# One layer on one core: projections on 512 columns, four and three counts in the top-k, first expert weights split on ScalarE and VectorE

## The chip, the core and the metric

The kernel runs on one core of a Trainium2 chip. The time is device microseconds of one execution. Of the kernel before, three runs gave 3871.36, 3886.71 and 3886.52 us, a median of 3886.52 us.

## The reference

One layer of a diffusion backbone: 2048 latent tokens and 256 context tokens of 1024 channels, all in float32. The line of computation that matters here:

```python
h_lat, h_ctx = modulate(layer_norm(x), sh1, sc1), modulate(layer_norm(ctx), mc[0], mc[1])
mix = token_mixer(h_lat, h_ctx, ...)     # p = h @ w_in; attention on part of p's columns,
                                         # RWKV-7 scans on the others; concat(...) @ w_out
x = layer_norm_affine(ALPHA * x + gt1 * mix, ln1_g, ln1_b)
h2 = modulate(layer_norm(x), sh2, sc2)
aff = softmax(h2 @ router_w)             # 2048 tokens x 16 experts
gate, idx = top_k(aff.T, 256)            # each expert takes its 256 best tokens
xin = h2[idx]                            # 16 x 256 x 1024
y = (silu(xin @ w_gate) * (xin @ w_up)) @ w_down
x = layer_norm_affine(ALPHA * x + gt2 * scatter_add(gate * y), ln2_g, ln2_b)
```

The six modulation vectors (sh1, sc1, ...) come from `silu(c) @ w_ada + b_ada`.

## The kernel before

**A product in float32** is made of three matmuls. `split` (its cast is at line 43 when it goes to ScalarE, at line 45 on GpSimd; its subtraction at line 48, on VectorE) makes of an operand a high part of fewer bits and a low part, the rest: `wh` and `wl` of weights `wf`, `hTh` and `hTl` of tokens, `xh` and `xl` of an expert's tokens. The product sums high x high, high x low and low x high over 8 blocks of 128 channels: 24 matmuls into one accumulator.

**Stages**, by the profiled execution. Up to some 660 us the input projection, then the mixers until 2383, the output projection until 2613, the router with its top-k until 2683, the gather of the first expert's tokens, sixteen experts to some 3696, 70 us each, and the last normalisation.

**Input projection.** Tokens come in 9 tiles of 256 (t = 0 is the context). `to_hT` transposes a tile (16 transposes, line 307), modulates it (line 315) and splits it into `hT` of 8 x 256 columns. Weights come in column pieces of 256. Seven pieces (p = 3 to 9) go through `piece_ch` channel by channel: for each of three groups of three tiles, each tile and each half of 128 weight columns, 24 matmuls on 256 token columns (line 460, the weights as stationary operand), then a copy into `raw` on ScalarE (line 472), and token shifts and stores from there. The other pieces go through `piece_tok` (line 422), with the tokens as stationary operand. `fill` puts small work between matmuls: the rest of the transposes, and the small products of the modulation weights (line 191), 16 blocks of which are loaded during this stage into the same buffers `wf` by the queue of SyncE, which also issues the pieces' weight loads and the stores (`rkl`, `wll`) of the pieces. A scheduler sets the order on each engine by priorities; each engine takes its work in that order.

**Output projection.** 16 tiles of 128 tokens; `proj` makes for each four accumulations of 24 matmuls on 256 columns of the weights (line 1508, `woh` and `wol`, the tokens `mh`, `ml` as stationary operand), two into each 512-column bank. VectorE and ScalarE normalise behind that, and 8 transposes per tile (line 1551) lead to the router's logits.

**Top-k.** Two searches (`largest`) of five rounds each find the 256th largest value for each expert, three bits a round. In a round, seven candidates are tried at once: VectorE counts for five (line 1689), ScalarE sums signs for two (line 1686); TensorE adds over partitions, the signs first (line 1695), then the counts (line 1696); VectorE makes of that the number of candidates that hold (line 1697), the next candidates (`tkcand`, line 1700, from `tkbase`, line 1692) and the threshold (line 1702). After the first search come lines 1716 and following.

**Experts.** Weights come in pieces of 1 MB into four buffers `wf` and are split into three buffers `wh`, `wl`; the pieces run gate, up, gate, up, ..., then four of down. `fetch` issues a load, `split` the split, `take` both, four and two pieces ahead. The first two pieces are fetched and split ahead of the first expert, the first four are loaded from 2626 us on. Pieces 0 and 1 are cast and subtracted on GpSimd, pieces 2 and 3 cast on ScalarE and subtracted on GpSimd (lines 1843 and 1844), the others go through `split` of line 43. `compact` and `gathered` make the first expert's list of tokens and fetch them.

## Time and profile before

| | us |
|---|---|
| median of three runs | 3886.52 |
| the profiled execution's own time | 3881.74 |
| its span | 3880.0 |
| TensorE busy | 3521.1 (91%) |
| VectorE busy | 2584.3 (67%) |
| ScalarE busy | 1714.7 (44%) |
| GpSimd busy | 1446.5 (37%) |

The profile is of one execution. Busy time is summed over the instructions of an engine; matmuls overlap, so the distance between their starts, not the duration in a row, is what one of them takes from the stream. The granted clock is a share of TensorE's higher level of 2.4 GHz. A chain of waits is followed back from the last instruction; where several instructions follow each other on one engine it gives them as one piece with their count. A row of the timeline gives start, duration, engine, line, operation, the tiles written and read with their shapes, and, in brackets, how long the engine had been idle and what released it.

### The profile page before, as it was taken

How to read it: one execution, taken by the hardware profiler on the slowest of the kernel's cores; microseconds unless marked ns; L12 is line 12 of the kernel's file. 1: busy time of each engine (PE TensorE's matmuls, PEld its weight loads, DVE VectorE, ACT ScalarE, POOL GpSimd, SP SyncE). 2: the span in 40 equal slices, each digit the busy share in tenths (PEclk: the TensorE clock that was granted, in tenths of full speed). 3: DMA queues.
4: the chain of work that ended last, by engine and by line, in shares of the span. 5: the costliest groups of instructions: out<-in, count | busy, mean ns of one | idle time of the engine just before them, and what ended most of it. 6: DMA issues, size and time to landing. Idle time of an engine off the chain costs nothing. (4 is left out here: it accounts for less than half of the span.)

```text
span 3880.0 us, 83041 instructions
## 1 busy us (share of the span) xinstructions
PE 3521.1 (91%) x34103; PEld 2969.3 (77%) x34103; DVE 2584.3 (67%) x4413; ACT 1714.7 (44%) x3255; POOL 1446.5 (37%) x1326
## 2 busy tenths in 40 slices
PE   7999898689998998899999999984999999999987
PEld 6888797466666666666777666983999999999976
DVE  5665646666766777676667766786565555556588
ACT  4544344344444444344454434543444444444443
POOL 3332322465655555565665541333101011011025
PEclk8999998799999999899999998996999999999988
DMA  7756544222232333333224324433667666666674
GB/s 230 240 177 189 161 154 144 65 65 69 71 84 71 91 94 90 90 83 77 68 70 101 83 54 155 149 124 128 216 206 211 213 205 209 213 211 212 211 270 165
DMA packets 635534, 554.78 MB, mean 143 GB/s; under 512 B 264113, under 2 KB 584145, under 8 KB 635153
## 3 DMA queue, kind: packets, MB, share of 16 engines
q1 hardware_dynamic: 622672, 505.94, 42.7%
q0 software_dynamic: 12480, 43.52, 4.8%
q8 instruction: 268, 4.39, 0.5%
q14 instruction: 114, 0.93, 0.1%
HBM read 428.28 MB, written 121.03 MB: 142 GB/s over the span
## 5 line engine op out<-in xcount | busy, mean ns | idle before, releaser
L904 POOL TENSOR_TENSOR acc<-acc,pt 128x512 f32<-128x512 f32 x496 | 660.2, 1331 | 352.4 <-ACT pt L876 327.4
L48 DVE TENSOR_TENSOR wl<-wf,wh 128x1024 fp32r<-128x1024 f32 x434 | 532.5, 1252 | 292.7 <-ACT wh L43 292.5
L1975 PE MATMUL gu<-xh,wl 128*128 128x256 f32 x2048 | 585.7, 286 | 20.9 <-DVE wl L48 20.9
L43 ACT CAST wh<-wf 128x1024 fp32r<-128x1024 f32 x434 | 440.6, 1046 | 333.2 <-issue 105.9
L1975 PE MATMUL gu<-xh,wh 128*128 128x256 f32 x2048 | 582.8, 285 | 0.9 <-DVE sg L1981 0.9
L1975 PE MATMUL gu<-xl,wh 128*128 128x256 f32 x2048 | 583.6, 285 | 0.0
L876 ACT ACTIVATE pt<-st 128x512 f32<-128x512 f32 x576 | 316.7, 595 | 389.9 <-PE st L872 359.5
L843 DVE TENSOR_REDUCE mx<-bk 128x1 f32<-128x512 f32 (+1 forms) x640 | 377.9, 627 | 154.8 <-PE bk L841 153.9
L1975 PEld LDWEIGHTS gu<-xh,wl 128*128 128x128 f32 x2048 | 391.0, 191 | 22.3 <-DVE wl L48 22.3
L1975 PEld LDWEIGHTS gu<-xh,wh 128*128 128x128 f32 x2048 | 392.2, 191 | 1.9 <-DVE sg L1981 1.1
L1975 PEld LDWEIGHTS gu<-xl,wh 128*128 128x128 f32 x2048 | 390.0, 190 | 0.6
L897 PE MATMUL po<-pt,vt 128*64 128x256 f32 x2304 | 320.2, 403 | 1.6 <-ACT pt L876 1.3
L2019 POOL DMA_INDIRECT acc<-ysb,idx x30 | 47.9, 1597 | 680.8 <-DVE ysb L2016 589.6
L460 PE MATMUL mm<-hTh,wh 128*128 128x256 f32 x968 | 281.8, 291 | 4.0 <-POOL raw L479 2.2
L460 PE MATMUL mm<-hTl,wh 128*128 128x256 f32 x968 | 278.8, 288 | 1.2 <-DVE hTl L48 1.2
L460 PE MATMUL mm<-hTh,wl 128*128 128x256 f32 x968 | 276.0, 285 | 0.0
L871 PE MATMUL st<-qs,k 128*128 128x512 f32 x576 | 250.2, 434 | 10.2 <-ACT pt L876 10.1
L872 PE MATMUL st<-q,kl 65*128 65x512 f32 x576 | 236.2, 410 | 11.7 <-DMA q<-mr 11.7
L841 PE MATMUL bk<-k,qs 128*128 128x512 f32 (+1 forms) x640 | 230.7, 440 | 16.5 <-DVE mx L843 7.3
L897 PEld LDWEIGHTS po<-pt,vt 128*64 128x64 f32 x2304 | 145.6, 140 | 104.1 <-issue 45.6
L460 PEld LDWEIGHTS mm<-hTh,wh 128*128 128x128 f32 x968 | 186.6, 193 | 12.4 <-issue 8.1
L460 PEld LDWEIGHTS mm<-hTl,wh 128*128 128x128 f32 x968 | 186.7, 193 | 6.2 <-issue 4.1
(431 smaller groups left out, 8298.7 us busy)
## 6 DMA issues: line engine op xcount, KB each, us to landing
wf<-in_exp_w_gate_dram SPq DMA_DIRECT2D x64, 1024.0 KB
wf<-in_exp_w_up_dram SPq DMA_DIRECT2D x64, 1024.0 KB
wf<-in_exp_w_down_dram SPq DMA_DIRECT2D x64, 1024.0 KB
win<-rkl SPq DMA_DIRECT2D x64, 512.0 KB
wf<-in_w_in_dram SPq DMA_DIRECT2D x30, 1024.0 KB
wf<-in_w_ada_dram SPq DMA_DIRECT2D x20, 1024.0 KB
wl<-wll SPq DMA_DIRECT2D x64, 256.0 KB
pwin<-rkl SPq DMA_DIRECT2D x32, 384.0 KB
```

The lines of the kernel that those rows point to most:

```text
L43: nc.scalar.copy(hi, src)
L48: nc.vector.tensor_sub(lo, src, hi)
L460: mm = nc.tensor.matmul(ps[:, c], a[:, k, cs], b[:, k], start=m == 0, stop=m == 3 * KD - 1)
L841: nc.tensor.matmul(ps[:, :n], qs[:, hh, i * 128:(i + 1) * 128], K2[j][:, c * 512:c * 512 + n], start=True, stop=True)
L843: nc.vector.reduce_max(mx[:, hh * 2 + i, c:c + 1], ps[:, :n], axis=AX.X)
L871: nc.tensor.matmul(st, K2[j][:, ksl], qs, start=True, stop=False)
L872: nc.tensor.matmul(st, KL[j][:, ksl], q2, start=False, stop=True)
L876: nc.scalar.activation(pt, st, AF.Exp, scale=0.125)
L897: nc.tensor.matmul(po[hh * 64:(hh + 1) * 64], VT[j][:, kt], pt[:, hh], start=kt == 0, stop=kt == KT - 1)
L904: add(acc, acc, pt)
L1975: mm = nc.tensor.matmul(ps[:, i], a[:, k, 128 * c:128 * c + 128], b[:, k], start=n == 0, stop=n == 3 * KD - 1)
L2019: nc.gpsimd.indirect_dma_start(out=self.acc, in_=y[h], in_offset=None, compute_op=ALU.add, out_offset=bass.IndirectOffsetOnAxis(ap=idx[h], ...
```

## The change

The input projection's tiles are grouped anew: `GROUPS` names in each of the three groups one tile alone and one pair. The two tiles of a pair lie side by side in one `hT` of 512 columns, and `piece_ch` runs their 24 matmuls on 512 columns (line 464 now) into one bank and copies the whole bank. The small work is put in after the fourth and the eighth block of channels, so that its number of places stays. The spare buffers for the first modulation weights are halves of the new `hT`. In the output projection, weights lie in two tiles of 512 columns and each accumulation runs on 512 (line 1528 now). In the top-k, VectorE counts for four candidates (line 1710 now) and ScalarE sums signs for three (line 1707 now). All expert weights go through `split`, and the first two pieces' splits are written behind the first expert's compaction.

```diff
+            GROUPS = [[(0,), (1, 2)], [(3, 4), (5,)], [(6, 7), (8,)]]
             def hslot(i):
-                return [(htop if i < 3 else hbot).tile([128, KD, 256], F32R, name=f"hT{n}{i}") for n in "hl"]
+
+                if i == 2:
+                    return [htop.tile([128, KD, 256], F32R, name=f"hT{n}2") for n in "hl"]
+                if i in (0, 3):
+                    pair[i] = [(hbot if i else htop).tile([128, KD, 512], F32R, name=f"hT{n}{i}") for n in "hl"]
+                j = i in (1, 4)
+                return [x[:, :, 256 * j:256 * j + 256] for x in pair[i - j]]
...
-                hi, lo = hslot((0, 1, 2, 3, 4, 2, 0, 1, 2)[t])
+                slot = (2, 0, 1, 3, 4, 2, 0, 1, 2)[t]
+                hi, lo = hslot(slot)
...
+                def chain(ps, c, hi, lo):
+                    cs = slice(c * 128, (c + 1) * 128)
+                    m = 0
+                    for k in range(KD):
+                        for a, b in ((wh, hi), (wh, lo), (wl, hi)):
+                            mm = nc.tensor.matmul(ps, a[:, k, cs], b[:, k], start=m == 0, stop=m == 3 * KD - 1)
+                            m += 1
+                        if k == KD - 1 or k == 3 and hi.shape[2] == 512:
+                            fill(mm)
+
+                for n, ts in enumerate(GROUPS[g]):
+                    o = 2 + (512 if n and g else 0)
+                    if len(ts) == 2:
+                        for c in range(2):
+                            ps = pmm.tile([128, 512], F32, name="mm")
+                            chain(ps, c, *H[ts])
+                            nc.scalar.copy(raw[c][:, o:o + 512], ps)
+                        continue
...
-                    for j in (2 * c, 2 * c + 1):
-                        n = 0
-                        o = ps[:, (j % 2) * 256:(j % 2) * 256 + 256]
-                        for k in range(KD):
-                            for a, b in ((hi, woh), (hi, wol), (lo, woh)):
-                                nc.tensor.matmul(o, a[:, k], b[j][:, k], start=n == 0, stop=n == 3 * KD - 1)
-                                n += 1
-                        yield
+                    n = 0
+                    for k in range(KD):
+                        for a, b in ((hi, woh), (hi, wol), (lo, woh)):
+                            nc.tensor.matmul(ps, a[:, k], b[c][:, k], start=n == 0, stop=n == 3 * KD - 1)
+                            n += 1
+                        if k % 4 == 3:
+                            yield
...
-                for j in range(5, 7):
+                for j in range(4, 7):
                     nc.scalar.activation(junks, dh, AF.Sign, bias=cand[:, j:j + 1], scale=-1.0,
...
-                for j in range(5):
+                for j in range(4):
                     nc.vector.tensor_scalar(junk, d, cand[:, j:j + 1], None, op0=ALU.is_ge, op1=ALU.add,
...
-                    if i < 4:
-                        (nc.gpsimd.tensor_copy if i < 2 else nc.scalar.copy)(hi[:, s], w[:, s])
-                        nc.gpsimd.tensor_sub(lo[:, s], w[:, s], hi[:, s])
-                    else:
-                        self.split(hi[:, s], lo[:, s], w[:, s])
+                    self.split(hi[:, s], lo[:, s], w[:, s])
...
-            for i in range(2):
-                split(i)
             c0 = compact(0)
             self.slots(slice(1, NE))
+
+            with tc.issue_after(self.last_compact.ins):
+                for i in range(2):
+                    split(i)
```

The compiled order shows three places where instructions moved. First TensorE at the start of the input projection; `hTh_412` and `hTl_413` are tile 1's `hT`, and `tp<-ident` are the transposes of tile 2, which the kernel before has among tile 1's matmuls:

```order
L307 MATMUL tp<-ident,hTl_150 128x128
L460 MATMUL mm<-hTl_413,wh 128x256
L460 MATMUL mm<-hTh_412,wl 128x256
L460 MATMUL mm<-hTh_412,wh 128x256
L307 MATMUL tp<-ident,hTl_150 128x128 x10
L460 MATMUL mm<-hTl_413,wh 128x256
L460 MATMUL mm<-hTh_412,wl 128x256
```

The same place now, where `hTh_180` and `hTl_181` are the context tile's and `hTh_410` and `hTl_411` the first pair's:

```order
L316 MATMUL tp<-ident,hTh_149 128x128
L464 MATMUL mm<-hTh_180,wh 128x256
L464 MATMUL mm<-hTl_181,wh 128x256
L464 MATMUL mm<-hTh_180,wl 128x256
L316 MATMUL tp<-ident,hTh_149 128x128 x15
L464 MATMUL mm<-hTh_410,wh 128x512 x2
L464 MATMUL mm<-hTh_180,wh 128x256
```

All sixteen transposes of the pair's second tile stand ahead of the pair's first matmul.

Then ScalarE from the softmax of the logits (`lg`) to the split of the first expert's tokens (`xh<-tpe`), before:

```order
L1629 ACTIVATE lg<-lg 128x256
L1686 ACTIVATE tkjs,tksgn<-tkdh,tkcand 128x256 x8
L1843 CAST wh<-wf 128x1024
L1686 ACTIVATE tkjs,tksgn<-tkdh,tkcand 128x256
L1843 CAST wh<-wf 128x1024
L1686 ACTIVATE tkjs,tksgn<-tkdh,tkcand 128x256 x11
L43 CAST xh<-tpe 128x512
```

and now, with three signs in a round:

```order
L1707 ACTIVATE tkjs,tksgn<-tkdh,tkcand 128x256
L43 CAST wh<-wf 128x1024
L1707 ACTIVATE tkjs,tksgn<-tkdh,tkcand 128x256
L43 CAST wh<-wf 128x1024
L1707 ACTIVATE tkjs,tksgn<-tkdh,tkcand 128x256 x2
L43 CAST wh<-wf 128x1024
L1707 ACTIVATE tkjs,tksgn<-tkdh,tkcand 128x256
L43 CAST wh<-wf 128x1024
L1707 ACTIVATE tkjs,tksgn<-tkdh,tkcand 128x256
L43 CAST wh<-wf 128x1024 x2
L1707 ACTIVATE tkjs,tksgn<-tkdh,tkcand 128x256 x24
L43 CAST xh<-tpe 128x512
```

The casts of the first three pieces, two each, stand in the first three rounds; none stands behind the last sign.

Last VectorE in the first three rounds, before:

```order
L1689 TENSOR_SCALAR tkj,tkcnt<-tkdig,tkcand 128x256 x4
L1697 SCALAR_TENSOR_TENSOR tkhit<-lgp,tkneed 128x8
L1700 SCALAR_TENSOR_TENSOR tkcand<-tkhit,tkbase 128x7
L1702 SCALAR_TENSOR_TENSOR tkthr_30814<-tkhit,tkthr_30814 128x1
L1689 TENSOR_SCALAR tkj,tkcnt<-tkdig,tkcand 128x256
L1692 SCALAR_TENSOR_TENSOR tkbase<-j_27914,tkthr_30814 128x7
```

and now, from the second round's counts into the third round:

```order
L1710 TENSOR_SCALAR tkj,tkcnt<-tkdig,tkcand 128x256 x3
L48 TENSOR_TENSOR wl<-wf,wh 128x1024 x2
L1718 SCALAR_TENSOR_TENSOR tkhit<-lgp,tkneed 128x7
L1721 SCALAR_TENSOR_TENSOR tkcand<-tkhit,tkbase 128x7
L1723 SCALAR_TENSOR_TENSOR tkthr_28982<-tkhit,tkthr_28982 128x1
L48 TENSOR_TENSOR wl<-wf,wh 128x1024
L1710 TENSOR_SCALAR tkj,tkcnt<-tkdig,tkcand 128x256
L1713 SCALAR_TENSOR_TENSOR tkbase<-j_26856,tkthr_28982 128x7
L48 TENSOR_TENSOR wl<-wf,wh 128x1024
```

Two subtractions of the weights' split stand in each of these rounds, in rounds 1 and 2 between the last count and the reading of the sums. On GpSimd no expert split is left.

## Rows read from the trace of the kernel before

**Rows 1.** The page: busy time by engine, and the split's subtraction (mean ns).

```profile
PE 3521.1 (91%) x34103; PEld 2969.3 (77%) x34103; DVE 2584.3 (67%) x4413; ACT 1714.7 (44%) x3255; POOL 1446.5 (37%) x1326
...
L48 DVE TENSOR_TENSOR wl<-wf,wh 128x1024 fp32r<-128x1024 f32 x434 | 532.5, 1252 | 292.7 <-ACT wh L43 292.5
```

**Rows 2.** Windows: length, busy PE, PEld, DVE, ACT, POOL, clock, DMA share, GB/s.

```profile
60.00:640.00 580.00, 538.36 (x4331) 506.03 (x4330) 354.82 (x614) 261.15 (x511) 177.46 (x315) 0.97 0.59 181
2400.00:2560.00 160.00, 159.69 (x1439) 156.18 (x1438) 126.14 (x223) 84.54 (x160) 55.97 (x22) 1.00 0.44 149
2580.00:2620.00 40.00, 27.80 (x240) 25.17 (x240) 36.34 (x77) 16.19 (x35) 9.83 (x4) 0.85 0.24 92
2630.00:2657.00 27.00, 4.71 (x15) 3.93 (x15) 24.07 (x77) 7.78 (x22) 17.77 (x10) 0.50 0.69 218
2697.00:3680.00 983.00, 983.00 (x7172) 921.89 (x7171) 582.56 (x725) 443.87 (x616) 102.77 (x57) 1.00 0.66 208
```

**Rows 3.** Chain of waits in the experts: start, us, engine, tile and line.

```profile
2751.29 15.68 PE y L2008 x69
2766.97 23.04 PE gu L1975 x192
```

**Rows 4.** Timeline of TensorE in the attention, first and last of four.

```profile
1002.53 0.40 PE L871 MATMUL st<-qs,k 128*128 128x512 f32 x1
...
1003.23 0.39 PE L872 MATMUL st<-q,kl 65*128 65x512 f32 x1
```

**Rows 5.** Groups of TensorE, input projection: busy us, mean ns, idle before, releasers.

```profile
L460 PE MATMUL mm<-hTh,wh 128*128 128x256 f32 x968 | 281.8, 291 | 4.0 <-POOL raw L479 2.2 <-POOL hTh L45 1.3 <-ACT wh L43 0.5
```

**Rows 6.** TensorE's waits 70 to 640 (us, times, longest), and line 191's instructions.

```profile
PE tp L191 <- DMA wf<-in_w_ada_dram: 9.6, 3, 5.9
...
L191 PE MATMUL tp<-wf,cst x256: 377/379/635, 133.9 to 447.2; 128*32 128x256 f32 x128
```

**Rows 7.** Timeline of TensorE at the start of the input projection.

```profile
64.38 0.38 PE L460 MATMUL mm<-hTh,wh 128*128 128x256 f32 x1 [2.15 <-POOL raw L479]
```

**Rows 8.** Timeline of VectorE in the top-k.

```profile
2631.02 0.47 DVE L1689 TENSOR_SCALAR_CACHE_REDUCE tkj<-tkdig,tkcand 128x256 int16<-128x256 int16 x1
...
2634.42 2.18 DVE L1700 SCALAR_TENSOR_TENSOR tkcand<-tkhit,tkbase 128x7 f32<-128x7 f32 x1
...
2636.64 0.48 DVE L1689 TENSOR_SCALAR_CACHE_REDUCE tkj<-tkdig,tkcand 128x256 int16<-128x256 int16 x1
...
2657.43 0.48 DVE L1716 TENSOR_SCALAR_CACHE_REDUCE tkj<-tkdig,tkthr 128x256 int16<-128x256 int16 x1
...
2666.17 0.17 DVE L1700 SCALAR_TENSOR_TENSOR tkcand<-tkhit,tkbase 128x7 f32<-128x7 f32 x1
...
2666.38 0.48 DVE L1689 TENSOR_SCALAR_CACHE_REDUCE tkj<-tkdig,tkcand 128x256 int16<-128x256 int16 x1
...
2669.90 0.48 DVE L1689 TENSOR_SCALAR_CACHE_REDUCE tkj<-tkdig,tkcand 128x256 int16<-128x256 int16 x1
```

**Rows 9.** Timeline of ScalarE in the top-k.

```profile
2653.65 1.03 ACT L1843 CAST wh<-wf 128x1024 fp32r<-128x1024 f32 x1
...
2666.43 0.51 ACT L1686 ACTIVATE tkjs<-tkdh,tkcand 128x256 bf16<-128x256 f32 x1 [2.29 <-DVE tkthr L1702]
...
2667.07 0.51 ACT L1686 ACTIVATE tkjs<-tkdh,tkcand 128x256 bf16<-128x256 f32 x1
```

**Rows 10.** Timeline of TensorE in the top-k.

```profile
2655.23 0.59 PE L1695 MATMUL lgp<-tksgn,samen 128*128 128x2 f32 x2 [3.84 <-ACT tkjs L1686]
2655.72 0.38 PE L1696 MATMUL lgp<-tkcnt,same 128*128 128x6 f32 x1
...
2667.72 0.59 PE L1695 MATMUL lgp<-tksgn,samen 128*128 128x2 f32 x2 [1.86 <-ACT tkjs L1686]
2669.01 0.38 PE L1696 MATMUL lgp<-tkcnt,same 128*128 128x6 f32 x1 [0.70 <-DVE tkj L1689]
```

**Rows 11.** Timeline of GpSimd in the top-k.

```profile
2632.26 2.02 POOL L1843 CAST wh<-wf 128x1024 fp32r<-128x1024 f32 x2 [6.52 <-DMA wf<-in_exp_w_gate_dram]
```

More of the change, by code (lines that the diff above doesn't have):

```diff
@@ L319, in to_hT @@
                 H[t] = (hi, lo)
+                if slot in (1, 4):
+                    H[t - 1, t] = pair[slot - 1]
                 if t == 0:
@@ L453, in piece_ch @@
                     ps = pmm.tile([128, 2, 256], F32, name="mm")
-                    before(n)
+                    before(2 if t else 0)
                     for c in halves:
-                        cs = slice(c * 128, (c + 1) * 128)
-                        m = 0
-                        for k in range(KD):
-                            for a, b in ((wh, hi), (wh, lo), (wl, hi)):
-                                mm = nc.tensor.matmul(ps[:, c], a[:, k, cs], b[:, k], start=m == 0,
-                                                      stop=m == 3 * KD - 1)
-                                m += 1
-                        fill(mm)
+                        chain(ps[:, c], c, *H[t])
                     for c in halves:
@@ L554, in inproj @@
             self.ada_bias()
-            spare = [hslot(3), hslot(4)]
+            hslot(3)
+            spare = pair[3]
             wb = [wpool.tile([128, KD, 256], F32, name="wf") for _ in range(2)]
-            wb += [w.bitcast(F32) for pair in spare for w in pair]
+            wb += [w.rearrange("p k n -> p (k n)")[:, 2048 * j:2048 * j + 2048].rearrange("p (k n) -> p k n", k=KD).bitcast(F32)
+                   for w in spare for j in range(2)]
             self.ada_load(0, wb[0])
@@ L1472, in outproj @@
                     nc.sync.dma_start(wf, I["w_out"][0].rearrange("(k p) n -> p k n", p=128)[:, :, j * 256:j * 256 + 256])
-                    for i, n in enumerate(("woh", "wol")):
-                        WO[i].append((first if j == 0 else wres if j == 1 else work).tile([128, KD, 256], F32R, name=f"{n}{j}", bufs=1))
+                    c, cs = j // 2, slice(256 * (j % 2), 256 * (j % 2) + 256)
+                    if j % 2 == 0:
+                        for i, n in enumerate(("woh", "wol")):
+                            WO[i].append((work if c else first).tile([128, KD, 512], F32R, name=f"{n}{c}", bufs=1))
                     for g in range(2):
                         ks = slice(4 * g, 4 * g + 4)
-                        self.split(WO[0][j][:, ks], WO[1][j][:, ks], wf[:, ks])
+                        self.split(WO[0][c][:, ks, cs], WO[1][c][:, ks, cs], wf[:, ks])
                     if j == 0:
@@ L1866, in compact @@
                 for t in range(16):
-                    nc.tensor.matmul(ps, oh[:, t], self.tok[:, :, t, e], start=t == 0, stop=t == 15)
+                    self.last_compact = nc.tensor.matmul(ps, oh[:, t], self.tok[:, :, t, e], start=t == 0, stop=t == 15)
                 idx = [work.tile([128, 1], I32, name=f"idx{h}", bufs=3) for h in range(2)]
```

30 lines of the change are left out of this document (12 added, 18 removed).

## The prediction

> **What bounds the kernel now.** I read the page first. TensorE is busy for 91% of the span, VectorE for 67% [rows 1]; that average says nothing yet on a single stage, so I asked for the stages' windows next. In the projections (60 to 640 us) TensorE is busy for 538.36 of 580.00 us at a granted clock of 0.97, in the body of the output projection for 159.69 of 160.00, in the experts for 983.00 of 983.00 [rows 2]. There a shorter instruction stream on TensorE shortens the stage. In the last 40 us of the output projection it is VectorE (36.34 of 40.00) that fills the time, and in the first rounds of the top-k TensorE has 4.71 us of work in 27.00 [rows 2]. The chain of waits agrees for the experts: nearly all of it there is TensorE at lines 1975 and 2008 [rows 3]. The mixers and the experts keep their instructions, so three places count: projections, output projection, top-k.
>
> **Half as many matmuls, each twice as wide.** What one matmul costs is the distance between starts, not its duration in the trace, since they overlap. The chain's pieces give it: 192 matmuls on 256 columns in 23.04 us are 120.0 ns each, 69 on 512 columns in 15.68 us are 227.2 ns each [rows 3]. Both are streams with a new stationary operand for every matmul, as the changed lines are. Two of the first less one of the second is 240.0 − 227.2 = 12.8 ns saved for each pair. Nearest row on the other side: in attention, where the stationary operand has 65 rows or 128 in turn, starts of 512-column matmuls at 2.4 GHz stand 0.23 us apart (the first of four at 1002.53, the last at 1003.23: 0.70 over 3, or 233 ns) [rows 4]. That leaves 7 ns. I take 12.8, because the row is the nearer in kind: one accumulation chain, full operands.
>
> **Projections.** Line 460 has 3 groups of 968 matmuls, one of them shown [rows 5]; of these, 7 column pieces x 3 groups x 2 tiles x 2 halves x 24 = 2016 are joined into 1008. 1008 x 12.8 = 12.9 us. TensorE idles for 580.00 − 538.36 = 41.6 us of this stage, 7% [rows 2], where others are late, and it would arrive at those waits earlier; I take twice that share, 2 us, as absorbed. Against it stands the start: a matmul of a pair needs both tiles, while in the kernel before tile 1 can start before tile 2 is turned. As the part on the change shows, the pair's first matmul follows all 16 transposes of tile 2, so tile 1's matmuls no longer run between them. TensorE now starts on tile 2's columns at 64.38 after 2.15 us without work [rows 7]; I price the loss at 1 us, between 0 (that idle time hides it) and 3.5 (2.15 once more, and the 1.3 us that groups at line 460 have in all for GpSimd's hT [rows 5]). The wider copies on ScalarE halve in number and hide behind TensorE: ScalarE is busy for 261.15 of 580.00 us [rows 2]; without this cover they would cost nothing more either, as the columns stay the same. 12.9 − 2 − 1 gives **−10**; ends −4 (7 ns, the full loss) and −13.
>
> **Output projection.** Line 1508 has 16 tiles x 4 x 24 = 1536 matmuls, which become 768: 768 x 12.8 = 9.8 us. The last two of 16 tiles lie where VectorE sets the time [rows 2], which takes off 2/16, 1.2 us; a little of the stage's start is at the lower clock, where I count no gain, 0.2. **−8.4**, ends −4 and −9.8. The wider tiles of split weights are the same bytes by the same splits.
>
> **Top-k.** A round of the second part starts its first count at 2666.38, the next at 2669.90: 3.52 us [rows 8]. In it the two signs' sums are ready 1.34 us after the start (2667.72), the counts 2.63 after (2669.01), and from the counts' matmul to the next round are 0.89 us [rows 8, 10]. With 4 counts of 0.53 (2.63 over 5) the counts end at 2.1. But a sign takes 0.64 (2666.43 to 2667.07 [rows 9]), three of them end near 2.0, and TensorE then has the signs' matmul ahead of the counts', 0.49 us (2655.23 to 2655.72 [rows 10]): 2.0 + 0.49 + 0.89 = 3.37. So the third sign takes back most of what the count gives, −0.15 us a round and not −0.53.
>
> The first part's first round takes 5.62 us, its five 26.41, from 2631.02 to 2657.43 [rows 8], and the reason is on view: GpSimd is splitting weights there (17.77 of 27.00 us busy [rows 2], from 2632.26 [rows 11]), and VectorE's 7-column operation at 2634.42 takes 2.18 us where the same takes 0.17 at 2666.17, with GpSimd quiet [rows 8]. Four rounds of 3.52 and a last one of 3.35, without those 0.17 for new candidates, would be 17.4: the splits cost 9.0. The change takes GpSimd out, but its words and its order differ: six casts on ScalarE and six subtractions on VectorE stand inside rounds 1 to 3, not at the gather. Their prices: a cast 1.03 [rows 9], a subtraction 1.25 [rows 1]. I follow the rounds. Round 1 starts at 2631.02; the second sign waits for a cast, whose weights were there by 2632.26 [rows 11]; cast, sign, cast, sign end at 2635.65, plus 0.49 and 0.89: 2637.0 where it was 2636.64, +0.4. Round 2 is three signs and two casts, 4.05 + 1.38, until 2642.45. Round 3 is bound by VectorE, two subtractions and four counts, 2.5 + 2.1, then 0.1 for the base, which follows the first count, and 0.89: 5.6, until 2648.05. Round 4 takes 3.37, until 2651.4, and round 5 3.2, until 2654.6 where it was 2657.43: **−2.8**. Five rounds of the second part give 5 x 0.15 = 0.75: **−3.6** in all. Ends: 0, if the weights land later than GpSimd's starts let see and block the signs behind the casts; −10.5, if the splits hide wholly (9.0 and 10 x 0.15). I take −3.6, because the durations that it adds up are rows of this stage, but for the subtraction's. The fourth piece is split beside the first expert's matmuls, now with VectorE's subtractions; VectorE is busy for 582.56 of 983.00 us there [rows 2], so that counts nothing, or two subtractions, 2.5 us, if they come late.
>
> **Sum.** −10 − 8.4 − 3.6 = −22 against the profiled execution's 3881.74: 3860 us. That execution stands 4.8 under the median 3886.52.
>
> **Rivals.**
> A: the splits in the rounds cost nothing, since ScalarE waits for thresholds in most of each round now (2.29 us before the sign at 2666.43 [rows 9]); top-k then gives its full 10.5, and 3881.74 − 10 − 8.4 − 10.5 = 3853. Against it: the casts stand between the signs that the round's sum needs.
> B: a 512-column matmul costs 233 ns [rows 4]. 7 ns a pair leave 1008 x 7 = 7.1, less 2 for waits, −5; 768 x 7 = 5.4, less 0.9, −4.5; with top-k's 3.6: 3868.6. For it: the row is of this kernel at the same clock; against it the longer stream of [rows 3]. The Trainium skill, "TensorE: Matmul & The Clock Gate", section "Back-to-back issue gap", gives an isolated matmul at full clock N / 2.4 + 2.5 ns. By it a pair saves 2.5 ns alone, an estimate of 4.4 us over 1776 pairs in place of 18.4, and the time would be close to B's. The rows at 120.0 and 227.2 speak against it for streams.
> C: the splits wait for their weight loads inside the rounds and top-k gains nothing: 3863.3. For it: ScalarE and VectorE work in order, so one late load holds signs and counts behind it; GpSimd was still waiting 6.52 us for the first of these at 2632.26 [rows 11].
> D, the other side: TensorE, which works in order, comes earlier to the small products of the modulation weights (line 191), whose loads stand in SyncE's queue behind the stores of the pieces. Three times it waits for them now, 9.6 us in all, 5.9 the longest [rows 6]. 256 matmuls are 16 to a block, 16 blocks [rows 6]; were each to wait the longest, that is 16 x 5.9 − 9.6 = 85 us more: 3881.74 − 22 + 85 = 3945. It decides from 3.2 us a block: 16 x 3.2 − 9.6 = 41.6 is what it takes to turn −22 into +19.4. Against it: 13 of 16 blocks find their load there now, and the stage gets shorter by 2% only.
>
> **How the numbers follow.** About 0.5%, 19.4 us, is what a measurement can tell from no change. The forecast (3853 to 3867 by its own ends) has 0.54, of which 0.45 lie beyond 0.5% and 0.09 within. A has 0.11, faster. B 0.14 and C 0.13, both within. D 0.08, slower. Faster 0.56, same 0.36, slower 0.08. All gains at their high ends (13, 9.8, 10.5) give 3848; all at their low ends (4, 4, 0) give 3874, and with the 4.8 between profiled run and median 3878. The range is 3848 to 3878.
>
> **What would show it.** Right: starts of line 464's and 1528's joined matmuls 227 ns apart; the projections some 10 us shorter from 60 to 640, the output projection's tile shorter by 48 x 12.8 ns, 0.6 us; rounds of the second part 3.37 apart and no 7-column operation on VectorE over 0.3 us. Wrong: 233 ns between those starts (B), casts in rounds 1 to 3 that idle for a load (C), rounds 1 to 3 near 3.4 us (A), or over 40 us more of waits at the modulation weights (D). A new wait at the experts' start, which I price at nothing since all six early splits precede it, would undo the rest.

## The result and the profile after

The changed kernel's median is 3861.8 us (six runs, 3851.06 to 3865.74), beside 3881.59 us for the kernel before in the same number of runs. The ratio is 0.9945, with a 95% interval from 0.9924 to 0.9966: some 21 us faster, by between 13 and 30. Two more series of the same kernel gave 0.9935 [0.9915, 0.9955] and 0.9941 [0.9925, 0.9958]. The forecast was 3860 us, with a range from 3848 to 3878. The sum held; two of its terms did not, and two places that it priced at nothing moved. The rest of this document is about that.

The page of the kernel after, its line of busy times (compare [rows 1]):

```profile
PE 3503.6 (91%) x32327; PEld 2869.7 (74%) x32327; DVE 2557.0 (66%) x4399; ACT 1727.4 (45%) x3239; POOL 1426.3 (37%) x1314
```

TensorE has 1776 matmuls fewer, as many as there are pairs. The windows of the kernel after (columns as in [rows 2]; in its span the stages begin 10 to 20 us earlier, so only the body of the projections and of the output projection can be laid beside the rows of before; the output projection's matmuls stand at line 1530 of the kernel after, not at 1528 as written above):

```profile
60.00:640.00 580.00, 545.36 (x3442) 469.21 (x3442) 360.42 (x639) 264.47 (x477) 179.62 (x318) 0.97 0.59 182
...
2400.00:2560.00 160.00, 153.36 (x862) 121.45 (x862) 113.61 (x230) 89.43 (x170) 58.13 (x23) 1.00 0.43 149
```

The second line is the surprise: where TensorE had been busy for 159.69 of 160.00 us, it is now busy for 153.36. It waits there now.

Laid out by stages, from the first and last instructions of the lines that mark them, in the two profiled executions:

| stretch | before, us | after, us | difference | forecast |
|---|---|---|---|---|
| start to the first attention matmul (line 871) | 679.6 | 669.8 | −9.8 | −10 |
| to the last attention matmul (line 897) | 1702.7 | 1699.7 | −3.0 | 0 |
| to the first transposes of the output projection | 39.9 | 37.6 | −2.3 | } |
| to its last transposes | 200.2 | 200.6 | +0.4 | } −8.4 |
| to the first count | 8.6 | 8.8 | +0.2 | 0 |
| first search (to line 1716) | 26.4 | 21.7 | −4.7 | −2.8 |
| to the first expert's indices | 28.5 | 27.1 | −1.4 | −0.75 |
| to the transposes of its tokens | 5.0 | 7.3 | +2.3 | 0 |
| to the end | 1189.1 | 1188.1 | −1.0 | 0 |
| **span** | **3880.0** | **3860.7** | **−19.3** | **−22** |

So the projections came out as forecast, the output projection gave 2 us in place of 8.4, the top-k gave more than forecast and lost part of it again at the gather.

**TensorE's new wait.** The list of what TensorE waits for in the kernel after, two rows from 40 to 670 us, then two from the output projection (us in all, times, longest):

```profile
PE tp L191 <- DMA wf<-in_w_ada_dram: 8.4, 3, 4.0
...
PE mm L464 <- POOL hTh L45: 4.0, 1, 4.0
...
PE tp L1574 <- ACT xh L1562: 12.1, 2, 7.1
PE tp L1574 <- ACT xh L1550: 7.4, 10, 0.8
```

The first row answers [rows 6]: the waits for the loads of the modulation weights did not grow. The second is the start of the first pair, which waits for tile 2, 4.0 us where it was 2.15 [rows 7]. The third, at the last tiles, was there before, with 12.2 us. The fourth has grown: ten tiles' transposes wait for ScalarE's normalised tile `xh`, nine of them for 0.77 to 0.79 us. In the kernel before that wait came to 1.2 us in all, over three tiles.

The timelines of one turn of that stage in the kernel after, of TensorE, ScalarE, VectorE and GpSimd:

```profile
2487.57 1.09 PE L1574 MATMUL tp<-ident,xh 128*128 128x128 f32 x8 [0.78 <-ACT xh L1550]
...
2501.45 1.09 PE L1574 MATMUL tp<-ident,xh 128*128 128x128 f32 x8 [0.79 <-ACT xh L1550]
```

```profile
2485.24 1.13 ACT L43 CAST mh<-mt 128x512 fp32r<-128x512 f32 x2
2486.28 1.24 ACT L1550 ACTIVATE xh<-x,mv 128x1024 f32<-128x1024 f32 x1
...
2491.86 1.25 ACT L1546 ACTIVATE u<-u,mv 128x1024 f32<-128x1024 f32 x1 [2.70 <-DVE mv L230]
```

```profile
2488.62 0.21 DVE L227 BATCH_NORM_AGGREGATE mv<-bnst 128x2 f32<-128x12 f32 x1
2490.27 1.23 DVE L1608 TENSOR_TENSOR h<-h,sh 128x1024 f32<-128x1024 f32 x1 [1.44 <-POOL h L1607]
2491.42 0.16 DVE L229 RECIPROCAL mv<-mv 128x1 f32<-128x1 f32 x1
...
2495.62 1.23 DVE L1548 TENSOR_TENSOR x<-x,b 128x1024 f32<-128x1024 f32 x1 [2.45 <-POOL x L1547]
```

```profile
2487.60 2.64 POOL L1607 TENSOR_TENSOR h<-xh,sc 128x1024 f32<-128x1024 f32 x1 [5.89 <-ACT xh L1550]
2493.18 2.40 POOL L1547 TENSOR_TENSOR x<-u,g 128x1024 f32<-128x1024 f32 x1 [2.94 <-ACT u L1546]
```

Read in order of time they are a ring. ScalarE makes `xh` (2486.28); GpSimd scales it (2487.60, 2.64 us); VectorE adds to that (2490.27) after waiting 1.44 us, and only behind this addition, in VectorE's order, stands the rest of the next tile's statistics (2491.42); on these waits ScalarE's `u` of the next tile (2491.86, after 2.70 us without work), on this GpSimd (2493.18), then VectorE (2495.62), and at last the next `xh`, 13.88 us after the one before. TensorE does not set the pace of this ring; it only waits for `xh`.

The change did not make this ring. It was there before, and it was slower. ScalarE's `xh` in the kernel before, the row of all thirteen of them (with the first and last start), and two in a row from the timeline:

```profile
L1527 ACT ACTIVATE xh<-x,mv x13: 1242/1244/1248, 2414.6 to 2582.8; 128x1024 f32<-128x1024 f32 x13
```

```profile
2498.60 1.24 ACT L1527 ACTIVATE xh<-x,mv 128x1024 f32<-128x1024 f32 x1
...
2512.65 1.25 ACT L1527 ACTIVATE xh<-x,mv 128x1024 f32<-128x1024 f32 x1
```

They mostly follow each other after 14.03 us (13.86 to 14.06 in this profile), while TensorE turns from tile to tile in 13.35. A head start hid the ring: the first tile's transposes came 6.4 us after the end of its `xh`; each tile used up 0.7 us of that, and from the eleventh tile on TensorE had to wait. In the kernel after, the first transposes come only 1.8 us behind their `xh`, and TensorE waits from the fourth tile on. The new order even made the ring shorter, by some 0.15 us: on ScalarE both casts of `mh` now stand ahead of `xh` (1.13 us in place of 0.60), but on VectorE the subtraction for `ml` that ran beside GpSimd's scaling, ahead of the addition, takes 0.68 us in place of 2.19.

**The top-k.** The timeline of VectorE in the kernel after, the first count of each round of the first search, the count behind it, and two rounds of the second:

```profile
2616.53 0.47 DVE L1710 TENSOR_SCALAR_CACHE_REDUCE tkj<-tkdig,tkcand 128x256 int16<-128x256 int16 x1
...
2621.35 0.17 DVE L1721 SCALAR_TENSOR_TENSOR tkcand<-tkhit,tkbase 128x7 f32<-128x7 f32 x1
2621.80 0.48 DVE L1710 TENSOR_SCALAR_CACHE_REDUCE tkj<-tkdig,tkcand 128x256 int16<-128x256 int16 x1 [0.21 <-DVE tkthr L1723]
...
2627.60 0.47 DVE L1710 TENSOR_SCALAR_CACHE_REDUCE tkj<-tkdig,tkcand 128x256 int16<-128x256 int16 x1
...
2631.68 0.48 DVE L1710 TENSOR_SCALAR_CACHE_REDUCE tkj<-tkdig,tkcand 128x256 int16<-128x256 int16 x1
...
2634.98 0.48 DVE L1710 TENSOR_SCALAR_CACHE_REDUCE tkj<-tkdig,tkcand 128x256 int16<-128x256 int16 x1
...
2638.19 0.48 DVE L1737 TENSOR_SCALAR_CACHE_REDUCE tkj<-tkdig,tkthr 128x256 int16<-128x256 int16 x1
...
2643.18 0.48 DVE L1710 TENSOR_SCALAR_CACHE_REDUCE tkj<-tkdig,tkcand 128x256 int16<-128x256 int16 x1
...
2646.48 0.48 DVE L1710 TENSOR_SCALAR_CACHE_REDUCE tkj<-tkdig,tkcand 128x256 int16<-128x256 int16 x1
```

The rounds take 5.27, 5.80, 4.08, 3.30 and 3.21 us, against 26.41 in all before [rows 8]; the 7-column operation at 2621.35 takes 0.17 us where it took 2.18. A round of the second search takes 3.30 us (2643.18 to 2646.48), against 3.52.

### The profile page after: what moved, and what is told of

Same layout as the page of the kernel before. It is cut to its first block, busy times and chain, and to the rows that moved or that the text cites. A ratio compares the mean times of both kernels' runs of the same rounds, so it can differ in the third digit from the quotient of the medians.

```text
span 3860.7 us, 79450 instructions
## 1 busy us (share of the span) xinstructions
PE 3503.6 (91%) x32327; PEld 2869.7 (74%) x32327; DVE 2557.0 (66%) x4399; ACT 1727.4 (45%) x3239; POOL 1426.3 (37%) x1314
## 5 line engine op out<-in xcount | busy, mean ns | idle before, releaser
L48 DVE TENSOR_TENSOR wl<-wf,wh 128x1024 fp32r<-128x1024 f32 x442 | 542.2, 1252 | 274.5 <-ACT wh L43 274.3
L43 ACT CAST wh<-wf 128x1024 fp32r<-128x1024 f32 x442 | 448.7, 1047 | 322.3 <-issue 103.3
L464 PE MATMUL mm<-hTh,wh 128*128 128x512 f32 (+1 forms) x632 | 225.3, 357 | 4.5 <-POOL hTh L45 4.0
L464 PE MATMUL mm<-hTl,wh 128*128 128x512 f32 (+1 forms) x632 | 219.9, 348 | 0.0
L464 PE MATMUL mm<-hTh,wl 128*128 128x512 f32 (+1 forms) x632 | 219.6, 348 | 0.0
L1890 POOL DMA_INDIRECT gat<-h2d,idx x32 | 62.1, 1941 | 306.0 <-DVE idx L1889 280.8
L863 PEld LDWEIGHTS bk<-k,qs 128*128 128x128 f32 x640 | 105.7, 196 | 78.5 <-issue 27.2
```

The source lines that it names most:

```text
L43: nc.scalar.copy(hi, src)
L48: nc.vector.tensor_sub(lo, src, hi)
L464: mm = nc.tensor.matmul(ps, a[:, k, cs], b[:, k], start=m == 0, stop=m == 3 * KD - 1)
L863: nc.tensor.matmul(ps[:, :n], qs[:, hh, i * 128:(i + 1) * 128], K2[j][:, c * 512:c * 512 + n], start=True, stop=True)
```

## The experiments

### Each part alone

**Pairs alone.** The kernel before with the new `GROUPS`, `hslot` and `piece_ch`:

```diff
+            GROUPS = [[(0,), (1, 2)], [(3, 4), (5,)], [(6, 7), (8,)]]
...
+                    if len(ts) == 2:
+                        for c in range(2):
+                            ps = pmm.tile([128, 512], F32, name="mm")
+                            chain(ps, c, *H[ts])
+                            nc.scalar.copy(raw[c][:, o:o + 512], ps)
+                        continue
```

> The kernel before with the pairing of the input projection's tiles alone. Theory: the whole gain of that part is there without the others, the first attention matmul (line 871) stands 9 to 11 us earlier than in the kernel before (679.6), and every later stage keeps its length, so the time is 9 to 11 us below the kernel before. Rival: the 3 us that the mixers were shorter in the changed kernel belong to this part too (stores and loads that come at other times), then the whole is 12 to 14 us. Other rival: those 3 us are spread between executions, then they are missing here or anywhere.

Measured: the first attention matmul at 666.5, 13.1 us earlier than in the profile of before, and a ratio of 0.9951 [0.9934, 0.9969], 12 to 26 us. The first is more than expected because the point that was compared with is itself not fixed: of six profiles without pairs the first attention matmul stands at 675.1 to 679.6 us (mean 678.0), of seven with pairs at 663.0 to 669.8 (mean 666.2). The difference of the means is 11.8 us, near the forecast's 10. The second is about twice the expected 9 to 11: the mixers were shorter by 16 us in this execution, 1686.9 us, of which the theory had nothing and the first rival 3; the run was therefore repeated (below).

**Wide output projection alone.** The kernel before with

```diff
-                    for j in (2 * c, 2 * c + 1):
-                        n = 0
-                        o = ps[:, (j % 2) * 256:(j % 2) * 256 + 256]
-                        for k in range(KD):
-                            for a, b in ((hi, woh), (hi, wol), (lo, woh)):
-                                nc.tensor.matmul(o, a[:, k], b[j][:, k], start=n == 0, stop=n == 3 * KD - 1)
+                    n = 0
+                    for k in range(KD):
+                        for a, b in ((hi, woh), (hi, wol), (lo, woh)):
+                            nc.tensor.matmul(ps, a[:, k], b[c][:, k], start=n == 0, stop=n == 3 * KD - 1)
```

> The kernel before with the 512-column output projection alone. Theory: the stage is limited by the chain from VectorE over ScalarE to the transposes of the normalised tile: two casts of the next tile's operand now stand ahead of that tile's last activation on ScalarE, TensorE waits 0.7 to 0.8 us for it in ten of sixteen tiles, and the stage gains 2 us, not 8.4. Rival: the loss comes from the different start of the stage in the changed kernel (the other parts moved it); then this kernel gains 6 to 8.4 us in the stage.

Measured: first transposes 2.4 us sooner after the mixers (37.5 against 39.9 us), first to last transposes 200.8 us, so 1.8 us for the stage, as the theory said. The ratio is 0.9982 [0.9962, 1.0003]. One row holds first and last transposes of this kernel:

```profile
L1552 PE MATMUL tp<-ident,xh x128: 270/273/476, 2416.5 to 2617.3; 128*128 128x128 f32 x128
```

The loss belongs to this part and not to what the other parts moved. The reason that the theory gives does not hold, though: with the two casts ahead of `xh` the ring takes 13.89 us here, less than the 14.03 of the kernel before.

**Splits alone**, with 5 counts and 2 signs as before:

```diff
-                    if i < 4:
-                        (nc.gpsimd.tensor_copy if i < 2 else nc.scalar.copy)(hi[:, s], w[:, s])
-                        nc.gpsimd.tensor_sub(lo[:, s], w[:, s], hi[:, s])
-                    else:
-                        self.split(hi[:, s], lo[:, s], w[:, s])
+                    self.split(hi[:, s], lo[:, s], w[:, s])
```

> The kernel before with the first expert weights' splits on ScalarE and VectorE alone, 5 counts and 2 signs as before. Theory: GpSimd next to the rounds was the price; the first search takes 21 to 22.5 us in place of 26.41, the second search stays at 3.52 us a round, 4 to 5 us in all. Rival: the counts are what gave the gain; then the first search stays over 25 us.

Measured: the first search takes 23.1 us, 3.3 less than before; the expected 21 to 22.5, and the 4 to 5 us in all, were too good. From the first search to the indices 28.9 us, as before (28.5), and from there to the transposes of the first expert's tokens 7.1 in place of 5.0. The ratio, 0.9993 [0.9976, 1.001], shows nothing. Most of the gain at the rounds is lost at the gather.

**Counts alone**, splits on GpSimd as before:

```diff
-                for j in range(5, 7):
+                for j in range(4, 7):
...
-                for j in range(5):
+                for j in range(4):
```

> The kernel before with 4 counts and 3 signs alone, splits on GpSimd as before. Theory: a round of the second search takes 3.30 us in place of 3.52 (ScalarE's third sign and the order of the two sums on TensorE set it), the first search gains 0.2 in a round at most since VectorE's 7-column operations still take 1.3 to 2.2 us beside GpSimd: 1 to 2 us in all. Rival: with one count less VectorE misses GpSimd's splits, and the first search gains 3 us or more.

Measured: the first search 25.4 us, 1.0 less; to the indices 27.1, 1.4 less; to the transposes 5.0, as before. VectorE's 7-column operations still stretch beside GpSimd, in the timeline of this kernel:

```profile
2632.48 2.03 DVE L1698 SCALAR_TENSOR_TENSOR tkcand<-tkhit,tkbase 128x7 f32<-128x7 f32 x1
...
2634.95 1.86 DVE L1690 SCALAR_TENSOR_TENSOR tkbase<-j,tkthr 128x7 f32<-128x7 f32 x1
```

So the two edits of the top-k are worth 2.9 (3.3 less 0.4) and 2.3 us there, 6.1 together in the changed kernel (4.7 and 1.4), and the splits cost 2.1 to 2.3 at the gather, which leaves 3.8.

### The output projection's ring

**First attempt: later transposes.** If TensorE waits for `xh`, let it ask later. The same kernel also tried whether the first gather is slow because GpSimd has been idle for 55 us:

```diff
-                    if j == (0 if last else 2) and t >= 2:
+                    if j == (0 if last else 3) and t >= 2:
                         turn(t - 2)
...
         largest(digit, dh, need, thrs[1])
+        nc.gpsimd.tensor_copy(sb([128, 256], F32, "tkpoke"), thrs[1].to_broadcast([128, 256]))
```

> The changed kernel with two edits. In the output projection a tile's transposes are written behind the fourth quarter of the next tiles' matmuls in place of the third; and GpSimd copies 256 columns once, after the second search, so that it has been idle some 10 us and not 55 when it issues the first gather. Theory: TensorE's wait of 0.7 to 0.8 us a tile for the normalised tile goes, and the stage takes the 6 us that it held back (first to last transposes near 194 us in place of 200.6); the gather's first issue takes about 1.1 us in place of 2.67 and the first expert starts 1.5 to 2.3 us earlier behind the indices. In all 7 to 8 us below the changed kernel. Rivals: the chain from VectorE over GpSimd and ScalarE has no slack itself, then the tile keeps its 13.9 us wherever the transposes stand; the gather's issue has to do with what was last issued, not with the idle time, then it stays at 2.67.

Measured: both theories fell. First to last transposes took 211.7 us, 11 more than in the changed kernel, a tile 15.09 us; the ratio to the kernel before rose to 0.9981 [0.9966, 0.9996]. The row that holds the first and last transposes of this kernel, and then its timeline of GpSimd:

```profile
L1574 PE MATMUL tp<-ident,xh x128: 270/272/477, 2398.3 to 2610.1; 128*128 128x128 f32 x128
```

```profile
2658.79 0.40 POOL L1745 COPY tkpoke<-tkthr 128x256 f32<-128x256 f32 x1 [45.38 <-DVE tkthr L1723]
2668.92 2.67 POOL L1891 DMA_INDIRECT gat<-h2d,idx  x1 [9.73 <-DVE idx L1890]
2671.90 0.97 POOL L1891 DMA_INDIRECT gat<-h2d,idx  x1 [0.30 <-issue]
```

After 9.73 us of idle time the first gather's issue takes the same 2.67 us as after 55.

**The control** with the kernel before, transposes one quarter later:

> The kernel before with the transposes of the output projection one quarter later, as a control. Theory: TensorE does not wait there in the kernel before (159.69 of 160.00 us busy), so the stage keeps 200 us, give or take 1. Rival: the placing is better in itself, then it gains 3 us or more here too.

Measured: 211.6 us there too, and a ratio of 1.0044 [1.0025, 1.0062]. Neither the theory nor the rival: the placing costs 11 us in either kernel. So the place of the transposes matters to the ring. On ScalarE the modulated copies (`h2T`, 2.90 us) that follow the transposes stand in one row with the next tile's work: in the timeline of the attempt they lie between `xh` (2477.76) and the next `u` (2485.02), while in the changed kernel they come behind that `u`. That they alone make the 11 us was not tried. The next edit shortens the ring instead.

**Second attempt: GpSimd out of the ring.** The 2.64 us of GpSimd between `xh` and VectorE's addition go to VectorE:

```diff
-            def rows_out(t, add):
+            def rows_out(t, add, mul=nc.gpsimd.tensor_mul):
...
-                nc.gpsimd.tensor_mul(h2, xh, rows["sc2"])
+                mul(h2, xh, rows["sc2"])
...
-                        rows_out(t - 3, nc.vector.tensor_add)
+                        rows_out(t - 3, nc.vector.tensor_add, nc.vector.tensor_mul)
```

> The changed kernel with one edit: in the output projection's loop the scaling of the normalised tile by the modulation (the first half of what rows_out writes) runs on VectorE and not on GpSimd. Theory: the stage turns at 13.9 us a tile in a loop that TensorE is not part of: the normalised tile on ScalarE, GpSimd's scaling of it (2.6 us), VectorE's addition behind that, which stands in VectorE's order ahead of the next tile's mean and scale, then ScalarE, GpSimd and VectorE for the next normalised tile. Without GpSimd's 2.6 us in it the loop has slack, TensorE no longer waits 0.7 to 0.8 us a tile, first to last transposes take 191 to 195 us in place of 200.6, and the time is 6 to 9 us below the changed kernel. Rival: VectorE, with 1.2 us more of work a tile, becomes the bound, and the stage keeps its length or grows.

Measured: first to last transposes 190.9 us, 9.8 less, a tile 13.05 us, and TensorE busy nearly throughout. Of this kernel the row of first and last transposes, the timeline's transposes of three tiles, and a window:

```profile
L1574 PE MATMUL tp<-ident,xh x128: 270/273/473, 2402.2 to 2593.1; 128*128 128x128 f32 x128
```

```profile
2480.55 1.09 PE L1574 MATMUL tp<-ident,xh 128*128 128x128 f32 x8 [0.24 <-ACT xh L1550]
2493.60 1.09 PE L1574 MATMUL tp<-ident,xh 128*128 128x128 f32 x8
2506.65 1.09 PE L1574 MATMUL tp<-ident,xh 128*128 128x128 f32 x8
```

```profile
2420.00:2540.00 120.00, 119.76 (x679) 94.51 (x678) 93.77 (x191) 71.90 (x141) 22.72 (x10) 1.00 0.45 160
```

The time is 3835.87 us, a ratio of 0.9898 [0.9878, 0.9918], where the changed kernel beside it had 0.9941: this version is the fastest of the series. The two ratios differ by 0.0043, 17 us, more than the expected 6 to 9; the stage explains 9.8 of them, the rest was not looked for, and the intervals are 13 and 16 us wide. The two profiled executions by themselves don't show the gain (spans of 3847.7 and 3843.1 us), because the mixers took 1699.5 us in this one and 1686.7 in the other; the section on the scatter of the mixers is about that.

**The control**, the same edit in the kernel before:

> The same edit in the kernel before, as a control. Theory: TensorE has no idle time in that stage (159.69 of 160.00 us busy), so first to last transposes stay at 200 us, within 1.5, the last tiles excepted. Rival: the edit is worth its 6 us without the wide matmuls too; then the loop was the bound before the change already.

Measured: 190.9 us here too, 9.3 less than before, with a ratio of 0.9978 [0.9964, 0.9992]. The rival was right, and where the theory erred shows in the tiles. Of this control the row of first and last transposes and the timeline's transposes of two tiles; behind them two tiles of the kernel before:

```profile
L1551 PE MATMUL tp<-ident,xh x128: 272/273/476, 2424.0 to 2614.9; 128*128 128x128 f32 x128
```

```profile
2503.90 1.04 PE L1551 MATMUL tp<-ident,xh 128*128 128x128 f32 x8
2517.25 1.04 PE L1551 MATMUL tp<-ident,xh 128*128 128x128 f32 x8
```

```profile
2502.12 1.04 PE L1551 MATMUL tp<-ident,xh 128*128 128x128 f32 x8
2515.47 1.03 PE L1551 MATMUL tp<-ident,xh 128*128 128x128 f32 x8
```

While TensorE does not wait, a tile takes 13.35 us with either placing of the scaling. The difference is at the end: in the kernel before the tiles from the tenth on take 13.82, 14.03, 14.03, 12.53, 11.85 and 12.44 us, in the control 13.35, 13.35, 13.35, 7.53, 9.31 and 12.45. With the scaling on VectorE the ring takes 13.05 us (between the third and the fifth `xh`), less than TensorE's 13.35, so TensorE leads to the end. In the kernel before the ring's 14.03 had caught up with it, and the waits, 4.79 us of them ahead of the fourteenth tile's transposes, put off the last matmul by 9.5 us.

What widening is worth to TensorE shows where nothing waits: in the changed kernel between the second and the third tile's transposes, ahead of the first wait:

```profile
2419.69 1.03 PE L1574 MATMUL tp<-ident,xh 128*128 128x128 f32 x8
...
2432.55 1.03 PE L1574 MATMUL tp<-ident,xh 128*128 128x128 f32 x8
```

That is 12.86 us in place of 13.35, so 0.49 us a tile, 10.2 ns for each of its 48 pairs. Three more profiles with the wide matmuls have the same 12.86. The 13.05 us of the version with the scaling on VectorE are not TensorE's own time yet. The view of ScalarE's `xh` in that kernel lists who waited for it (us, times):

```profile
  PEld tp L1574: 5.0, 12
```

In twelve tiles the loads ahead of the transposes (PEld) still waited for `xh`, although TensorE is shown as busy for 119.76 of 120.00 us. The shortened ring still leads there, by 0.19 us a tile. From the last attention matmul on, widening gives 2.2 us with the ring shortened, all of it ahead of the first transposes (37.5 against 39.7 us); from there both take 190.9 us.

### The scatter of the mixers

The changed kernel twice more and the pairs alone once more, with no edit:

> The changed kernel once more, beside the others on the same chip. The stage lengths of the first profile come back within 1 us for the output projection (200.6) and both searches (21.7 and 27.1); the mixers, whose clock is low for between 204 and 232 us in the six profiles so far, may differ by up to 15 us. The time is 15 to 25 us below the kernel before.

> The paired projections alone, once more. If the mixers' 1686.9 us came with the code (other moments for loads and stores), they are under 1690 again; if they came with the clock that this one execution was granted, they lie between 1697 and 1705 as in the five other profiles.

> The changed kernel a third time, beside its variant on the same chip. First to last transposes in the output projection 200.6 us within 0.5, the first search 21.7, from the indices to the first expert's transposes 7.2; the mixers between 1686 and 1703 us.

The stage lengths came back: the output projection 200.7 and 200.7 us, the first search 21.7 and 21.7, indices to transposes 7.2 and 7.1. The mixers took 1686.2 and 1686.7 us in the changed kernel, after 1699.7 in its first profile, and 1691.0 in the pairs alone, after 1686.9: between the two values that were to be told apart. The ratios are 0.9935, 0.9941 and, for the pairs alone, 0.9947 [0.9929, 0.9966]; the first median is 29 us below that of the kernel before, outside the expected 15 to 25, while its ratio gives 25.

The pairs alone thus have nearly the whole of the measured gain (0.9951 and 0.9947, beside 0.9945, 0.9935 and 0.9941 with all parts), and about half of it stands in the mixers, whose instructions they leave as they were.

Over all profiles the mixers take 1699.4 to 1705.6 us without the pairs (six, mean 1702.3) and 1686.2 to 1699.7 with them (seven, mean 1691.9), with the same 19143 matmuls on TensorE in all thirteen, in the same order but for one or two swapped neighbours. Cut into 48 stretches of 400 matmuls, ten agree to 0.1 us over all thirteen, and several take one of two or three values. One of these takes 34.1 to 34.2 us in seven profiles and 38.6 to 38.8 in six, with and without the pairs in both groups. Windows around it, in the kernel before and in the kernel with the splits alone (columns as in [rows 2]):

```profile
2254.00:2300.00 46.00, 43.73 (x457) 31.40 (x459) 26.89 (x60) 14.70 (x30) 14.79 (x13) 0.82 0.25 58
```

```profile
2250.00:2296.00 46.00, 41.21 (x497) 29.80 (x497) 32.31 (x70) 15.02 (x31) 18.60 (x15) 0.96 0.25 59
```

A granted clock of 0.82 against 0.96 in the same place of the program, and 457 matmuls done against 497. Over all stretches, each taken against its mean, the time at the lower level goes with the length (correlation 0.87, 0.37 us for each microsecond at 1.2 GHz). From the first to the last attention matmul it comes to 177 to 215 us; the 204 to 232 us of the expectation are counted from 640 to 2400 us. The kernels with pairs have some 9 us less of that on average (192 against 201), which by that slope is 3 to 4 of the 10 us. Whether the pairs are the cause is not shown: the two ranges meet. Why these executions have less, and where the rest is, stays open.

## Why the prediction was right, and where it was not

**Right: one pair saves 12.8 ns in the projections.** Between neighbouring matmuls of one form, leaving out gaps over 0.3 us, the distance of starts averages 121.1 ns on 256 columns in the kernel before (2553 of them, 70 to 600 us) and 229.4 ns on 512 in the kernel after (865): 2 x 121.1 − 229.4 = 12.8 ns. The term of −10 measured −9.8 in the two profiles, −11.8 between the means. The start was dearer than priced: the pair's wait for tile 2 is 4.0 us against 2.15, so 1.85 in place of 1. By the Trainium skill's formula for an isolated matmul ("TensorE: Matmul & The Clock Gate", "Back-to-back issue gap") a pair would save an estimated 2.5 ns; the rows of this kernel do not bear it out for streams, and the measurement decides.

**Wrong: that TensorE, busy for 159.69 of 160.00 us in the body of the output projection, sets the length of that stage ("There a shorter instruction stream on TensorE shortens the stage").** That is the step that failed. The row is right, but it says only that TensorE did not stop, not that the others kept up. A ring over ScalarE, GpSimd and VectorE took 14.03 us a tile in the kernel before, against TensorE's 13.35, and a head start of 6.4 us hid it for ten tiles. It takes 13.88 us in the changed kernel, where TensorE would need 12.86. So the term of −8.4 measured −1.9 (−2.3 at the start, +0.4 in the stage), and the tiles that others held up were not the last two, as the prediction has it, but six before the change and twelve after it. Without the ring a pair saves 10.2 ns here, 0.49 us a tile where 0.6 was forecast: between rival B's 7 ns and the 12.8. One cause is in the timeline: behind an interposed small matmul the next start comes 0.34 us later on 512 columns (2483.74 to 2484.08 in the kernel after), and on 256 columns the two next ones come after 0.22 and 0.12 (2485.80 to 2486.02 and 2486.14 before), so that pair saves next to nothing.

**Too small: the top-k.** −3.6 was forecast, −6.1 measured (−4.7 and −1.4). The reason given holds: GpSimd beside VectorE was the price, the third sign limits a round, 3.30 us against the forecast 3.37 and the 3.00 that counts alone would allow. The Trainium skill ("GPSIMD Engine Reference", "1. Specifications") has GpSimd share its memory interfaces with VectorE, with contention for VectorE's instructions with two inputs there; the rows agree: the 7-column operations, which have two, took 2.18 us (before) and 1.86 (counts alone) beside GpSimd and 0.17 without, while the counts, with one tensor, took 0.48 in either case [rows 8]. The mis-sized piece is the splits inside the rounds. Round 1 was forecast at 5.98 us and took 5.27, since the first weights were there by 2617.19, 0.66 us after the first count, where 1.24 had been assumed; round 3 was forecast at 5.6 and took 4.08, since its two casts ran ahead of its start, and one of its subtractions ahead of its first count, within round 2 (5.80 against 5.45). ScalarE's row for that first cast:

```profile
2617.19 1.04 ACT L43 CAST wh<-wf 128x1024 fp32r<-128x1024 f32 x1 [0.35 <-DMA wf<-in_exp_w_gate_dram]
```

Rival C, late loads, is thereby out: 0.35 us is what the loads cost. Rival A, no cost at all, is out by 5.27 and 5.80 against 3.30.

**Not foreseen: the gather.** "A new wait at the experts' start, which I price at nothing" was the right place to look and the wrong price: +2.3 us. GpSimd's timeline at the first gather, before and after:

```profile
2686.38 1.07 POOL L1873 DMA_INDIRECT gat<-h2d,idx  x1 [29.29 <-DVE idx L1872]
2687.76 1.78 POOL L1873 DMA_INDIRECT gat<-h2d,idx  x1 [0.30 <-issue]
```

```profile
2666.36 2.67 POOL L1890 DMA_INDIRECT gat<-h2d,idx  x1 [55.33 <-DVE idx L1889]
2669.34 0.96 POOL L1890 DMA_INDIRECT gat<-h2d,idx  x1 [0.30 <-issue]
```

The gather takes its longer course in every kernel that has no expert splits on GpSimd (7.0 to 7.2 us from indices to transposes in six profiles) and its shorter one in every kernel that has them (4.8 to 5.0 in seven). Idle time is not the cause, as the copy 9.73 us ahead of it showed. VectorE's timeline shows what runs beside the gather, an operation on two tensors for the experts' lists (`oh`), before and after:

```profile
2686.39 2.31 DVE L1862 TENSOR_TENSOR oh<-cid,slot 128x2048 f16<-128x2048 f16 x1
```

```profile
2665.81 2.28 DVE L1879 TENSOR_TENSOR oh<-cid,slot 128x2048 f16<-128x2048 f16 x1
```

Before, the first issue starts 0.01 us ahead of that operation and takes 1.07 us, and the second, which falls beside it, takes 1.78. After, the first starts 0.55 us behind its beginning and takes 2.67, and the second, behind its end, takes 0.96. In all thirteen profiles the issue that falls beside VectorE's operation ends 0.8 to 0.9 us after it. So the order of the two seems to decide the course; that is read from the timelines, and no edit tested it. Why the gather starts some 0.57 us later behind the indices in the kernels without GpSimd's splits stays open.

**Not foreseen: the mixers.** They were priced at nothing and were 3.0 us shorter in the profile, 10.4 between the means. That the sum came out is luck: the gain was right to within 3 us (19.3 against 22) because errors of +6.5 (output projection), −2.5 (top-k), +2.3 (gather) and −3 (mixers) nearly cancelled. With the means for the first two stages the change gives 11.8 + 10.4 + 1.9 + 3.8 = 27.9 us, which the intervals of the three series just hold (the first reaches 29.5).

**Rival D** (waits for the modulation weights' loads) did not happen: 8.4 us against 9.6. A smaller relative of it did: the product that follows them (line 212), which waits for a bias to be loaded and added, held TensorE for 14.7 us in place of 8.8. What that costs was not looked for.

## What to carry to other kernels

A busy share of 100% names the engine that does not stop, not the one that sets the pace: a head start can hide a slower ring for many tiles. Before a shorter stream on that engine is counted, follow one tile's result through the other engines in their own order, take the time from one tile to the next there, and compare it with the full engine's. If the ring is within the gain, the gain ends there; if it is already the longer one, there is next to none, and the cheaper edit may be to take one engine out of the ring (here one multiplication moved from GpSimd to VectorE, 9.3 us in the stage without any wider matmul). When a stage is changed by few microseconds, compare stage by stage: the mixers of these kernels, unchanged, scatter by more than two of the change's parts are worth.

## What the runs showed of the hardware

- The granted clock in the same place of the same instruction stream differs between executions: 0.82 or 0.96 over 46 us, and 177 to 215 us at the lower level over the mixers, whose length goes from 1686.2 to 1705.6 us.
- The first gather's issue took 1.07 us on GpSimd when it started just ahead of VectorE's 2.3 us operation on two tensors, and 2.67 when it started 0.55 us behind its beginning; the second issue took 1.78 beside it and 0.96 behind it. How long GpSimd had been idle made no difference (9.73 or 55 us, both 2.67).
- VectorE's 128x512 subtraction took 0.68 us alone and 2.20 beside a GpSimd operation on two tensors (2486.90 in the kernel before), about as long as GpSimd's, 2.68.
- Joining two matmuls of 256 columns into one of 512 saved 12.8 ns in the projections and 10.2 ns in a turn of the output projection in which nothing waited. Behind a small matmul of another shape the next start came 0.34 us later on 512 columns, and 0.22 on 256.
